# Layer 1's value projection for four head pairs in one 512-column pass at the layer junction, the keys' copied half on VectorE, and background sums held one step

## The chip, the cores and the metric

The kernel runs on one core of a Trainium2 chip. The metric is the device time of one execution in microseconds (us); lower is better. Engines are named as the profile names them: PE is TensorE (matmuls; PEld is its weight load), DVE is VectorE, ACT is ScalarE, POOL is GpSimd, and SP is SyncE, which here only issues the DMA transfers. Each engine works through its own instructions strictly in their order; between engines there are only semaphores.

## The reference

Two decoder layers on a residual stream of 512 tokens by 1024, float32, 16 heads of 64. Layer 0 has stick-breaking attention, layer 1 forgetting attention. Cut to what matters here:

```python
h = modulate(rmsnorm(x, g_mix_pre[i]), sh_a, sc_a)
q, k, v = (split_heads(t) for t in split(h @ w_qkv[i], 3))     # w_qkv: 1024 x 3072
if i == 0:
    o = stick_breaking_attention(q, k, v)
else:
    log_f = log_sigmoid(h @ w_fg + b_fg)                       # 16 columns
    o = softmax(q.k * scale + cum[t] - cum[s], causal) @ v     # cum = cumsum(log_f)
x = x + gt_a * rmsnorm(o @ w_o[i], g_mix_post[i])
h = modulate(rmsnorm(x, g_ffn_pre[i]), sh_f, sc_f)
x = x + gt_f * rmsnorm((silu(conv3(h @ w_gate)) * (h @ w_up)) @ w_down, g_ffn_post[i])
```

The six vectors `sh_a ... gt_f` of a layer are `silu(c) @ w_mod[i] + b_mod[i]`, each a 1024 x 1024 product with one vector.

## The kernel before

**Arithmetic.** To keep float32 accuracy every operand is split into a rounded high part and a low part (`split`, L245: ACT copies, then DVE or POOL subtracts), and a product is three matmuls into one PSUM bank (`mm3`, L318): high by high (L320), high by low (L321), low by high (L322). All are 128 x 128 weights against at most 512 moving columns.

**Weights.** One list (`ws`, L289) has every weight tile of the program in the order in which it is needed. A tile is 512 KB: a load into `wf` (three buffers) from SP, then its split into `wh` and `wl` (three buffers each, `w_tile`), or into four 128 x 512 pieces of the pool `slot` (`w_slots`; 44 slots, shared with attention's tiles and the feed-forward's results `ys`). Asking for a tile (`ws.need`) also issues the next ones, two ahead where nothing else is said. Of the qkv and output weights the low parts are made by POOL, of the feed-forward weights by DVE.

**Order.** PE and SP run in the order of the Python code. DVE, ACT and POOL are put in order by a scheduler when the program is built; only layer 0's start is in code order there too.

**The junction.** Layer 0 ends with the down projection. Its last four weight tiles are kept in slots and run token block by token block (four blocks of 128), so that a block's norms (`postnorm`, then `scaled`, each with a power of -0.5 on POOL, L333) run while the next block is multiplied. `finish_next` turns a finished block into layer 1's input `ht` (8 transposes on PE into `pt`, L373, then ACT and DVE). Layer 1 then begins with the values of head pairs 0 and 1 (`values`, group 0: 256 columns, for each block 8 x 3 matmuls of 256 moving columns), mixed with the last two blocks' transposes (`ready(2)`, `ready(3)`), the first half of q of pair 0, the forget gates (`forget`, 16 matmuls into `pf`, then a chain over ACT, DVE, a DRAM buffer `cumd` and the tiles `cum`), the rest of q (L835) and k (L836) of pair 0. The values of group 1 (pairs 2 and 3) come later, among the fillers.

**Attention.** `attention` (L574) works head by head; `UNITS` (L32) says for each head how many filler units (three matmuls of 512 columns, or six of 256) PE runs between its scores, transposes and sums. The fillers are the projections of the next pairs, values of later groups, and parts of the output projection. `keys` (L426) makes k of a pair: ACT rounds each head's half into `kh` (L431), POOL copies that half to the other 64 partitions (L433), DVE makes the low half `kl` (L434).

**Background sums.** During the feed-forward of layer 0 six modulation vectors are computed as background (`mod_part`, L133): eight loads `wm` from the pool `t4` (three buffers), each followed by a DVE multiply-add into `acc` (L144, L146); then `acc` is split into `ah` (ACT, L149) and `al` (DVE, L151), both in `t4` as well, and four matmuls `pm` (L163, L164) sum over partitions. `bg.step(4)` after each of the 22 feed-forward blocks (L928) runs four yields of this.

## Time and profile before

| what | value |
|---|---|
| time, median of 3 runs (lowest to highest) | 1272.24 us (1270.95 to 1272.52) |
| the profiled execution's own time | 1271.76 us |
| its span, first to last instruction | 1270.0 us |
| granted TensorE clock, mean | 0.999 |
| PE busy | 1246.4 us, 98% of the span |
| PEld, DVE, ACT, POOL busy | 81%, 54%, 47%, 21% |

The profiled execution is 0.48 us below the median; 1.8 us of its time lie outside the span. Matmuls overlap in the profile: a matmul of 512 columns is shown as some 0.39 us long while the next one starts 0.23 us after it. So what a matmul costs is the distance between starts, and an idle time shown in brackets hides a further 0.16 us (0.39 - 0.23) of lost spacing. The kernel is computed by PE almost without a pause, so its time is PE's spacing plus the few places where PE waits.

### The profile page before, as it was taken

The numbers are of one execution on the slowest core, as the hardware profiler recorded it, in microseconds if no ns is written. First come the engines' busy times: TensorE is split into PE (matmuls) and PEld (weight loads), VectorE is DVE, ScalarE is ACT, GpSimd is POOL, SyncE is SP. The second block draws the span as 40 slices with busy tenths as digits, with TensorE's granted clock in tenths as the row PEclk, the third lists the DMA queues.
The fourth block names the chain that finished last, engine by engine and source line by source line (L and its number), as shares of the span: only waits on it lengthen the run. The fifth ranks groups of instructions, "written<-read, shape, count | busy, mean of one in ns | idle before, by whom it ended". The sixth has DMA issues, their size and how long they took to land.

```text
span 1270.0 us, 17006 instructions
## 1 busy us (share of the span) xinstructions
PE 1246.4 (98%) x6380; PEld 1026.5 (81%) x6380; DVE 681.3 (54%) x1157; ACT 601.6 (47%) x1149; POOL 267.5 (21%) x302
## 2 busy tenths in 40 slices
PE   6999999999999999999999999999999999999997
PEld 5877878789887888888887888877988888888886
DVE  6655444377688887422263654554685444442233
ACT  7577667565333334311375655565743333332121
POOL 5764444610000000000215554352000000000000
PEclk9999999999999999999999999999999999999999
DMA  9746334324587875333504443233073333332331
GB/s 298 216 145 218 124 93 157 100 67 167 166 249 225 267 217 170 91 95 98 151 1 130 122 133 115 90 128 101 22 244 102 98 100 100 100 96 89 97 100 67
DMA packets 178357, 169.71 MB, mean 134 GB/s; under 512 B 6983, under 2 KB 151775, under 8 KB 178274
## 3 DMA queue, kind: packets, MB, share of 16 engines
q1 hardware_dynamic: 178098, 168.56, 43.5%
q8 instruction: 50, 0.82, 0.3%
q14 instruction: 33, 0.27, 0.1%
q10 hardware_dynamic: 176, 0.07, 0.0%
HBM read 166.44 MB, written 2.16 MB: 133 GB/s over the span
## 4 chain that ended last, share of the span: by engine, by line
PE 83%; DVE 6%; DMA 4%; ACT 4%; issue 1%; POOL 1%; SPq 0%; DVEq 0%; ACTq 0%; POOLq 0%
PE pgu L321 11%; PE pgu L322 11%; PE pgu L320 11%; PE pd L322 6%; PE pd L321 6%; PE pd L320 6%; PE pqk L320 4%; PE pqk L322 4%; PE pqk L321 4%; PE ps L442 3%; PE po L493 3%; PE pv L320 3%; PE pa L478 3%; PE pv L321 3%; PE pv L322 3%; DMA wf<-in_w_ffn_up_dram 2%
## 5 line engine op out<-in xcount | busy, mean ns | idle before, releaser
L246 ACT CAST wh<-wf 128x1024 fp32r<-128x1024 f32 (+2 forms) x178 | 185.3, 1041 | 307.6 <-PE pd L322 134.4
L321 PE MATMUL pgu<-htl,wh 128*128 128x512 f32 (+1 forms) x736 | 276.4, 376 | 0.6 <-DVE htl L382 0.6
L320 PE MATMUL pgu<-hth,wh 128*128 128x512 f32 (+1 forms) x736 | 276.3, 375 | 0.0
L322 PE MATMUL pgu<-hth,wl 128*128 128x512 f32 (+1 forms) x736 | 276.1, 375 | 0.0
L247 DVE TENSOR_TENSOR wl<-wf,wh 128x1024 fp32r<-128x1024 f32 x122 | 149.2, 1223 | 214.5 <-ACT wh L246 212.2
L321 PEld LDWEIGHTS pgu<-htl,wh 128*128 128x128 f32 x736 | 138.5, 188 | 26.2 <-DVE htl L382 1.0
L322 PEld LDWEIGHTS pgu<-hth,wl 128*128 128x128 f32 x736 | 138.5, 188 | 24.9
L320 PEld LDWEIGHTS pgu<-hth,wh 128*128 128x128 f32 x736 | 138.5, 188 | 24.9
L247 POOL TENSOR_TENSOR wl<-wf,wh 128x1024 fp32r<-128x1024 f32 (+3 forms) x56 | 129.7, 2320 | 122.4 <-ACT wh L246 101.6
L333 POOL TENSOR_TENSOR r<-v,mhalf 128x1 f32<-128x1 f32 x32 | 17.6, 551 | 450.5 <-DVE v L329 450.5
L320 PE MATMUL pd<-wh,yh 128*128 128x512 f32 x288 | 112.0, 389 | 0.0
L321 PE MATMUL pd<-wl,yh 128*128 128x512 f32 x288 | 112.0, 389 | 0.0
L322 PE MATMUL pd<-wh,yl 128*128 128x512 f32 x288 | 112.0, 389 | 0.0
L320 PE MATMUL pqk<-hth,wh 128*128 128x512 f32 (+1 forms) x240 | 99.6, 415 | 0.0
L322 PE MATMUL pqk<-hth,wl 128*128 128x512 f32 (+1 forms) x240 | 92.6, 386 | 0.9 <-POOL wl L247 0.9
L321 PE MATMUL pqk<-htl,wh 128*128 128x512 f32 (+1 forms) x240 | 92.5, 385 | 0.0
L904 ACT ACTIVATE cv<-cv 128x512 f32<-128x512 f32 x44 | 27.8, 632 | 111.1 <-DVE cv L903 103.8
L146 DVE SCALAR_TENSOR_TENSOR acc<-wm,csil,acc 128x1024 f32<-128x1024 f32 x52 | 66.6, 1281 | 16.5 <-DMA wm<-in_w_mod_dram 16.0
L320 PE MATMUL pv<-wh,hth 128*128 128x256 f32 (+1 forms) x224 | 70.8, 316 | 1.2 <-ACT hth L690 1.2
L322 PE MATMUL pv<-wh,htl 128*128 128x256 f32 (+1 forms) x224 | 66.9, 299 | 0.0
L321 PE MATMUL pv<-wl,hth 128*128 128x256 f32 (+1 forms) x224 | 66.7, 298 | 0.0
L321 PEld LDWEIGHTS pd<-wl,yh 128*128 128x128 f32 x288 | 54.1, 188 | 11.3
(208 smaller groups left out, 2241.0 us busy)
## 6 DMA issues: line engine op xcount, KB each, us to landing
wm<-in_w_mod_dram SPq DMA_DIRECT2D x80, 512.0 KB, 6.1
wf<-in_w_ffn_gate_dram SPq DMA_DIRECT2D x44, 512.0 KB, 4.9
wf<-in_w_ffn_up_dram SPq DMA_DIRECT2D x44, 512.0 KB, 4.7
wf<-in_w_ffn_down_dram SPq DMA_DIRECT2D x44, 512.0 KB, 3.5
wf<-in_w_qkv_dram SPq DMA_DIRECT2D x41, 512.0 KB, 5.8
wm<-in_w_mod_dram SPq DMA_DIRECT2D x32, 256.0 KB, 5.7
wf<-in_w_o_dram SPq DMA_DIRECT2D x16, 512.0 KB, 3.6
cum<-cumd SPq DMA_DIRECT2D x16, 512.0 KB, 5.4
```

Source lines behind the costliest of these rows:

```text
L146: nc.vector.scalar_tensor_tensor(acc, w, csil[:, d : d + 1], acc, op0=ALU.mult, op1=ALU.add)
L246: nc.scalar.copy(hi, src)
L247: (engine or nc.vector).tensor_tensor(lo, src, hi.bitcast(F32), op=ALU.subtract)
L320: nc.tensor.matmul(ps, ah, bh, start=first, stop=False)
L321: nc.tensor.matmul(ps, ah, bl, start=False, stop=False)
L322: nc.tensor.matmul(ps, al, bh, start=False, stop=last)
L333: nc.gpsimd.tensor_tensor(r, v, mhalf, op=ALU.pow)
L442: nc.tensor.matmul(ps[:, :n], q[hd][:, qs], k[hd][i][:, :n], start=i == 0, stop=i == 1)
L478: nc.tensor.transpose(ps[:, (qb - kb) * P : (qb - kb + 1) * P], probs[qb][:, kb * P : (kb + 1) * P], idn)
L493: nc.tensor.matmul(po[HD * hd : HD * hd + HD, kb * P :], vt[p // 4, kb][:, e : e + HD], at[hd][kb], start=kb == 0, stop=kb == NT - 1, tile ...
L904: nc.scalar.activation(a, a, AF.Silu)
```

## The change

Four parts.

1. **Values of four pairs.** In layer 1, groups 0 and 1 become one projection of 512 columns (`values4`): for each block 8 x 3 matmuls of 512 moving columns, its weights loaded as four tiles into 16 slots with the low parts on POOL. The order at the junction becomes values of block 0, transposes of block 2, values of block 1, transposes of block 3, values of block 2, forget gates, all of q and k of pair 0 (no longer in two halves), values of block 3. The four loads are asked for earlier (at block 1 of the down projection's end), and the two `ws.need` calls with 0 ahead limit how far the list runs on.
2. **Fillers.** Without group 1 there are 16 filler units fewer, and layer 1's `UNITS` go from 185 to 169 in sum, 18 to 14 for head 0, 12 to 10 or 11 for heads 1 to 8.
3. **Keys.** In both layers DVE fills the other 64 partitions of `kh` straight from PSUM; POOL's copy is gone.
4. **Background sums.** After `ah` and `al` the part yields `True`, which ends the step. So `pm` stands behind the next feed-forward block on PE. A part takes three steps where it took 2.75.

```diff
-         [18, 12, 12, 12, 12, 12, 13, 12, 12, 12, 11, 9, 10, 10, 4, 9, 5]]
+         [14, 10, 10, 10, 10, 11, 11, 11, 12, 12, 11, 9, 10, 10, 4, 9, 5]]
...
             res = cst.tile([P, ND], F32, name=nm("mc"))
-        yield
+        yield True
         for h in range(2):
...
         def step(self, n=1):
+
             while n and self.gens:
                 try:
-                    next(self.gens[0])
-                    n -= 1
+                    n = 0 if next(self.gens[0]) else n - 1
                 except StopIteration:
                     self.gens.pop(0)
...
-            vs = [((l, "v", p // 2, i), wq[:, 4 * i : 4 * i + 4, 2 * D + p * P : 2 * D + p * P + 256], 256) for i in range(2) if p % 2 == 0]
+            vs = [((l, "v", p // 2, i), wq[:, 4 * i : 4 * i + 4, 2 * D + p * P : 2 * D + p * P + 256], 256) for i in range(2) if p in (4, 6)]
+            if (l, p) == (1, 0):
+                for i in range(4):
+                    src = wq[:, 2 * i : 2 * i + 2, 2 * D : 2 * D + 512]
+                    ws.add((l, "v4", i), lambda src=src: w_slots(src, 512, nc.gpsimd))
...
         for (hi, lo), own, other in zip(res, (A, B), (B, A)):
-            nc.gpsimd.tensor_scalar(hi[other], hi[own].bitcast(F32), 1.0, 1.0, op0=ALU.mult, op1=ALU.mult)
+            nc.vector.tensor_copy(hi[other], ps[own])
             nc.vector.tensor_tensor(lo[own], ps[own], hi[own].bitcast(F32), op=ALU.subtract)
...
+    def values4(l, t, ht, vt):
+
+        ps = bank("pv")
+        for d in range(ND):
+            w = ws.need((l, "v4", d // 2), 4 - d // 2)
+            mm3(ps, block(ht, d, t * P, (t + 1) * P), w[d % 2], d == 0, d == ND - 1)
+        vt[0, t] = slot("v", F32)
+        nc.scalar.copy(vt[0, t], ps)
...
         else:
-            drain(values(l, 0, 0, ht, vt))
+            values4(l, 0, ht, vt)
             ready(2)
-            drain(values(l, 0, 1, ht, vt))
-            first = proj(l, 0, 0, ht, scale, qk, ((0, 256), (256, 512)))
-            for _ in range(4):
-                next(first)
+            ws.need((l, "qk", 0, 1), 0)
+            values4(l, 1, ht, vt)
             ready(3)
-            drain(values(l, 0, 2, ht, vt))
-            if l % 2:
-                cums_of[l] = forget(ht)
-            drain(values(l, 0, 3, ht, vt))
-            drain(first)
-            drain(proj(l, 0, 1, ht, None, qk))
+            ws.need((l, "qk", 1, 0), 0)
+            values4(l, 2, ht, vt)
+            cums_of[l] = forget(ht)
+            for j, s in ((0, scale), (1, None)):
+                drain(proj(l, 0, j, ht, s, qk))
+            values4(l, 3, ht, vt)
...
-            if p % 2 == 0 and p >= (4 if l == 0 else 2):
+            if p in (4, 6):
                 gens += [values(l, p // 2, t, ht, vt) for t in range(NT)]
...
                 xn[t] = scaled(t)
+                if t == 1:
+                    ws.need((l + 1, "v4", 3), 0)
```

What the built program's order shows at three places (names are the program's with their numbers; line numbers of the changed kernel are 4 to 13 higher).

POOL at the end of layer 0's down projection, before: `wl` are the low parts of the first three qkv tiles, `kl` the cleared key tiles, `r_1169` and `r_1175` the first two powers of -0.5, for block 0's norms.

```order
L423 MEMSET kl_1230_6011 64x512
L423 MEMSET kl_1231_6012 64x512
L423 MEMSET kl_1232_6013 64x512
L423 MEMSET kl_1233_6014 64x512
L247 TENSOR_TENSOR wl_1158_5754<-wf_1156_5751,wh_1157_5753 128x1024
L247 TENSOR_TENSOR wl_1161_5766<-wf_1159_5763,wh_1160_5765 128x1024
L247 TENSOR_TENSOR wl_1236_6022<-wf_1234_6019,wh_1235_6021 128x1024
L333 TENSOR_TENSOR r_1169_5787<-v_1168_5785,mhalf_78 128x1
L333 TENSOR_TENSOR r_1175_5799<-v_1174_5797,mhalf_78 128x1
```

The same place now; six more `sl` (low parts of the four value tiles) stand ahead of the first row.

```order
L247 TENSOR_TENSOR sl_1203_5878<-wf_1201_5875,sh_1202_5877 128x512
L247 TENSOR_TENSOR sl_1205_5882<-wf_1201_5875,sh_1204_5881 128x512
L427 MEMSET kl_1244_6039 64x512
L427 MEMSET kl_1245_6040 64x512
L247 TENSOR_TENSOR wl_1251_6051<-wf_1249_6048,wh_1250_6050 128x1024
L427 MEMSET kl_1246_6041 64x512
L427 MEMSET kl_1247_6042 64x512
L247 TENSOR_TENSOR wl_1259_6107<-wf_1257_6104,wh_1258_6106 128x1024
L247 TENSOR_TENSOR wl_1268_6164<-wf_1266_6161,wh_1267_6163 128x1024
L337 TENSOR_TENSOR r_1173_5795<-v_1172_5793,mhalf_78 128x1
```

Block 0's first power stands behind eight half tiles, three whole ones and four clears, where it stood behind three whole tiles.

POOL at k of pair 7 in layer 0, before, with what each instruction waits for:

```order
L247 TENSOR_TENSOR wl_554_2532<-wf_552_2529,wh_553_2531 128x1024 [waits PE_49,DMAHW3_49,Activation_49,Pool_49]
L433 TENSOR_SCALAR kh_548_2519<-kh_548_2519 64x512 [waits Activation_49,Pool_49]
L433 TENSOR_SCALAR kh_549_2520<-kh_549_2520 64x512 [waits Activation_49]
L247 TENSOR_TENSOR sl_558_2551<-wf_556_2548,sh_557_2550 128x512 [waits DMAHW4_49,Activation_49,Pool_49]
L247 TENSOR_TENSOR sl_560_2555<-wf_556_2548,sh_559_2554 128x512 [waits Activation_49]
```

DVE at the same k now:

```order
L437 CAST kh_548_2519<-pqk_528_2424 64x512 [waits PE_49,Activation_49]
L438 TENSOR_TENSOR kl_6_101<-pqk_528_2424,kh_548_2519 64x512
L437 CAST kh_549_2520<-pqk_528_2424 64x512
L438 TENSOR_TENSOR kl_7_102<-pqk_528_2424,kh_549_2520 64x512
L221 TENSOR_REDUCE mc_438_2002<-pm_555_2541 128x4 [waits PE_49]
```

The copy has moved from behind a weight's low part on POOL to DVE, where the two low halves stood alone, and it waits for ACT.

SP in layer 0's feed-forward around the first background sum, before (`gp` is loaded at the yield behind `ah` and `al`, `wm` is the next part's):

```order
L156 DMA gp_785_3671<-in_g_ffn_post_dram 128x1024
L142 DMA wm_789_3682<-in_w_mod_dram 128x1024
L252 DMA wf_792_3687<-in_w_ffn_gate_dram 128x8x128
L252 DMA wf_795_3717<-in_w_ffn_up_dram 128x8x128
L142 DMA wm_801_3757<-in_w_mod_dram 128x1024
L142 DMA wm_802_3760<-in_w_mod_dram 128x1024
L142 DMA wm_803_3763<-in_w_mod_dram 128x1024
L142 DMA wm_804_3766<-in_w_mod_dram 128x1024
```

The same place now:

```order
L156 DMA gp_785_3671<-in_g_ffn_post_dram 128x1024
L252 DMA wf_788_3675<-in_w_ffn_gate_dram 128x8x128
L252 DMA wf_791_3705<-in_w_ffn_up_dram 128x8x128
L142 DMA wm_800_3754<-in_w_mod_dram 128x1024
L142 DMA wm_801_3757<-in_w_mod_dram 128x1024
L252 DMA wf_804_3762<-in_w_ffn_gate_dram 128x8x128
L252 DMA wf_807_3792<-in_w_ffn_up_dram 128x8x128
L142 DMA wm_813_3832<-in_w_mod_dram 128x1024
```

One feed-forward block's two weight loads now come ahead of the next part's first `wm`, which came ahead of them.

## Rows read from the trace of the kernel before

**Rows 1.** The page, part 1: busy time of each engine.
```profile
PE 1246.4 (98%) x6380; PEld 1026.5 (81%) x6380; DVE 681.3 (54%) x1157; ACT 601.6 (47%) x1149; POOL 267.5 (21%) x302
```

**Rows 2.** PE's timeline: start, us, operation, [idle before <- what ended it].
```profile
224.18 0.50 PE L442 MATMUL ps<-kh,qa 128*128 128x512 f32 x1 [1.58 <-POOL kh L433]
...
393.55 0.50 PE L163 MATMUL pm<-ah,ones 128*128 128x512 f32 x1 [0.40 <-ACT ah L149]
395.39 0.50 PE L164 MATMUL pm<-al,ones 128*128 128x512 f32 x1 [1.34 <-DVE al L151]
...
661.62 1.09 PE L373 MATMUL pt<-zid,xn 128*128 128x128 f32 x8 [0.76 <-DVE xn L363]
...
681.94 0.50 PE L442 MATMUL ps<-kh,qa 128*128 128x512 f32 x1 [1.45 <-POOL kh L433]
682.49 0.50 PE L442 MATMUL ps<-kl,qa 128*128 128x512 f32 x1
...
696.04 0.50 PE L322 MATMUL pqk<-hth,wl 128*128 128x512 f32 x1 [0.86 <-POOL wl L247]
```

**Rows 3.** PE's timeline: 512-column matmuls, then 256-column ones, without waits.
```profile
642.69 0.39 PE L320 MATMUL pd<-sh,yh 128*128 128x512 f32 x1
...
647.00 0.39 PE L321 MATMUL pd<-sl,yh 128*128 128x512 f32 x1
...
651.06 0.28 PE L320 MATMUL pv<-wh,hth 128*128 128x256 f32 x1
...
653.82 0.28 PE L322 MATMUL pv<-wh,htl 128*128 128x256 f32 x1
```

**Rows 4.** POOL's and DVE's timelines at pair 7's keys, layer 0.
```profile
221.06 2.37 POOL L247 TENSOR_TENSOR wl<-wf,wh 128x1024 fp32r<-128x1024 f32 x1 [2.52 <-ACT wh L246]
223.51 1.31 POOL L433 TENSOR_SCALAR kh<-kh 64x512 fp32r<-64x512 f32 x2
...
222.05 1.41 DVE L434 TENSOR_TENSOR kl<-pqk,kh 64x512 fp32r<-64x512 f32 x2 [1.95 <-ACT kh L431]
```

**Rows 5.** DVE's groups by form, from PSUM and from SBUF.
```profile
L434 DVE TENSOR_TENSOR kl<-pqk,kh 64x512 fp32r<-64x512 f32 x30 | 20.6, 687 | 10.1 <-ACT kh L431 9.7
L381 DVE CAST hth<-hf 128x512 fp32r<-128x512 f32 x12 | 5.1, 422 | 4.5 <-ACT hf L378 4.5
```

**Rows 6.** The waits: engine, operation <- waited for: us in total, times, longest.
```profile
DVE u L388 <- ACT junk L341: 34.6, 8, 14.0
```

**Rows 7.** POOL's groups by form.
```profile
L247 POOL TENSOR_TENSOR wl<-wf,wh 128x1024 fp32r<-128x1024 f32 x47 | 112.6, 2402 | 116.8 <-ACT wh L246 96.6 <-PE pa L478 8.8 <-PE pv L321 5.6
L247 POOL TENSOR_TENSOR sl<-wf,sh 128x512 fp32r<-128x512 f32 x20 | 25.4, 1297 | 19.3 <-ACT sh L246 17.2 <-issue 1.9
...
L423 POOL MEMSET kl<- 64x512 f32 x8 | 4.2, 524 | 95.2 <-PE pd L321 94.9
```

**Rows 8.** ACT's timeline: the first qkv tile of layer 1 has landed.
```profile
619.94 1.05 ACT L246 CAST wh<-wf 128x1024 fp32r<-128x1024 f32 x1 [1.50 <-DMA wf<-in_w_qkv_dram]
```

**Rows 9.** POOL's, DVE's and PE's timelines: block 0 at the junction.
```profile
634.77 0.55 POOL L333 TENSOR_TENSOR r<-v,mhalf 128x1 f32<-128x1 f32 x1 [3.53 <-DVE v L329]
...
638.54 0.88 DVE L363 TENSOR_SCALAR xn<-xs,r 128x512 f32<-128x512 f32 x2 [0.67 <-POOL r L333]
...
641.12 1.03 PE L373 MATMUL pt<-zid,xn 128*128 128x128 f32 x8
```

**Rows 10.** DVE's timeline: layer 1's first softmax row block.
```profile
689.63 0.69 DVE L463 CUSTOM_DVE_ANT_0 fx<-ps,cum 128x512 f32<-128x512 f32 x1 [6.47 <-POOL cum L549]
```

**Rows 11.** Layer 0's feed-forward: a stretch (us, busy of PE, PEld, DVE, ACT, POOL, clock, DMA).
```profile
380.00:400.00 20.00, 18.26 (x80) 14.57 (x79) 18.08 (x26) 7.07 (x9) 0.00 (x0) 1.00 0.75 222
```

**Rows 12.** DVE's timeline and the DMA issues (count, KB each, median us to landing).
```profile
399.04 1.22 DVE L247 TENSOR_TENSOR wl<-wf,wh 128x1024 fp32r<-128x1024 f32 x1
...
wm<-in_w_mod_dram SPq DMA_DIRECT2D x80, 512.0 KB, 6.1
wf<-in_w_ffn_gate_dram SPq DMA_DIRECT2D x44, 512.0 KB, 4.9
```

## The prediction

> **What bounds the kernel now.** I read the page first: PE is busy 1246.4 us of a span of 1270.0, and no other engine over 54% [rows 1]. So a change gains only by shortening what PE has to do or by removing one of its pauses. The 23.6 us of pause are few and large; I looked for them in PE's timeline. About 9 us lie in layer 0's start and 7 at the very end, which this change does not touch. The rest, but for three of about 0.3 us, is in [rows 2]: a wait for POOL's copied half of k at pair 7 of layer 0 and again at pair 0 of layer 1, a wait for a background sum's `ah` and `al`, one for block 3's `xn` at the junction, one for a weight's low part early in layer 1's attention. As the section on the profile says, each costs its bracket and 0.16 of hidden spacing.
>
> **1. Width.** In [rows 3] the two 512-column matmuls are 19 starts apart, 4.31/19 = 0.227 us each; the two 256-column ones 23 starts apart, 2.76/23 = 0.120. Groups 0 and 1 of the values were 2 x 96 = 192 matmuls of 256 and become 96 of 512: 192 x 0.120 - 96 x 0.227 = 23.04 - 21.79 = **1.25**. The first q loses its halves: 48 x 0.120 - 24 x 0.227 = **0.31**. Nothing hides these, PE is the bound: 1.56 gained. By the Trainium skill (TensorE: Matmul & The Clock Gate, Back-to-back issue gap) a warm matmul's spacing is its columns at 2.4 GHz and about 2.5 ns, which is 109 and 216 ns. By that rule both terms would be 0.3 together; this trace has 120 and 227, and the measured spacing decides.
>
> **2. The junction's order.** Between block 2's and block 3's transposes stand 5.45 us of values now (24 x 0.227), where 24 + 24 matmuls of 256 stood (5.76), but block 2's come 2.57 later than before behind block 0's values, and block 3's chain no longer has block 2's subtraction of 1.1 us ahead of it on DVE. The wait for `xn`, 0.76 + 0.16 = **0.92** [rows 2], should go; behind it nothing is late. If block 3 is late by all that block 2's new place gives, up to 0.9 comes back.
>
> **3. Keys.** At pair 0 of layer 1 the scores waited 1.45 + 0.16, and 682.49 - 681.94 - 0.227 = 0.32 for `kl` [rows 2]. Now 5.45 us of block 3's values stand between k's projection and the scores. DVE needs four operations, at most 4 x 0.69 = 2.8, behind ACT's two copies: hidden, **1.93** gained.
> At pair 7 of layer 0 nothing new stands between. POOL's copies began at 223.51, behind a weight's low part that ran from 221.06 [rows 4]; DVE was free for `kl` at 222.05. The new copy isn't in the trace. Its bounds are DVE's 0.69 from PSUM and 0.42 for a cast from SBUF [rows 5]; I take 0.69, since it reads the same bank in the same shape. `kh` is ready at 222.74 and `kl` at 223.44, so the second score matmul starts there and not at 224.18 + 0.34: **1.07** gained; with 0.42 it is 1.34. The copy waits for ACT's two copies of the same bank, as DVE's product waits for ACT's square of the same bank elsewhere [rows 6]. The Trainium skill (PSUM — Partial Sum Buffer, PSUM bank collisions raise a hardware error) says why: two engines must not touch one bank in the same 32 partitions at once, two reads included. By that rule the gain is the 1.07; if the two could read together the whole wait of 1.74 would go. The row bears the rule out.
> In all other pairs PE did not wait for k, and DVE's 2 x 0.69 a pair lie beside fillers; an uncovered one would cost at most 0.7.
>
> **4. Background sums.** `pm` waited 0.40 + 0.16 and then 395.39 - 393.55 - 0.227 = 1.61: **2.17** [rows 2]. A feed-forward block is 48 x 0.227 = 10.9 us of PE, so a sum that is asked for one block later is there. What would be late next: the weights. DVE is busy 18 of 20 us there [rows 11], and the next block's second tile gets its low part at 399.04 + 1.22 = 400.26 [rows 12]; PE asked for it one tile of 24 matmuls and the brackets after `pm`, 395.39 + 0.34 + 24 x 0.227 + 0.45 = 401.6, and would 2.17 earlier, at 399.4. So between 0 and 2.17 stays. A part now takes three steps and not 2.75, so DVE and the DMA have 8% less background work in a block; I take the whole, 2.17.
>
> **5. Fillers.** The 16 units of group 1 move from attention to the junction; their cost is in part 1. Heads get some 1.4 us shorter. The heads behind the eighth had 9 to 11 units before and no pause over 0.35, so nothing for that. The wait of 0.86 + 0.16 = **1.02** for a low part [rows 2] came because head 0 ran 18 units, two of them with pair 2's q; now it runs 14, of pair 1 alone, and that tile has a head more. Against it, `forget` comes later: three times 5.45 - 2.88, less 2.88 of q and the 0.92, is 3.9, and 3.3 from part 6. The first softmax then starts not at 689.63 [rows 10] but near 696.8. PE starts head 0 some 10.7 later too, and its transposes need the rows a head later. I cost this at 0, up to 1 if the chain is slower.
>
> **6. What it costs: POOL at the junction.** The order shows that POOL does all low parts of four value tiles and three q and k tiles, and four clears, before block 0's first power: 8 x 1.297 + 3 x 2.402 + 4 x 0.524 = 19.7 us [rows 7]. It can't start sooner than the first tile lands, 619.94 [rows 8], and ACT's half copy is done, about 620.5: SP's first three loads wait for buffers of the down projection as before. So the power comes at 640.2 and not at 634.77 [rows 9], 5.4 later. From the power to the first half of `xn` the chain took 638.54 + 0.44 - 634.77 = 4.2, so PE can transpose block 0 at 644.4, where it did at 641.12. PE loses **3.3**. The later blocks' chains follow at the distances they had and just fit. The ends: 2.9 if POOL is a little quicker, 5 if it also waits for tiles.
>
> **Sum.** 1.56 + 0.92 + 1.93 + 1.07 + 2.17 + 1.02 = 8.67 gained, 3.3 lost, 5.4 net. Against the profiled execution's 1271.76 that is 1266.4; against the median, 0.48 above it, **1266.8 us**.
>
> **The rivals.**
> *POOL's queue is hidden after all.* If the tiles are split earlier than the rows allow, or block 0 has more room, the 3.3 do not come: 1272.24 - 8.7 = 1263.5. For it: `xn` of block 0 was ready 2.1 us ahead of PE [rows 9] (638.98 against 641.12), so a delay up to that costs nothing. Against it: POOL's work alone is 19.7 us behind a landing that the trace gives.
> *The pause only moves.* The sum's wait becomes a wait for weights (400.26 against 399.4, part 4), or the chains behind POOL miss by another one or two microseconds: 2 to 4 of the gain go, 1269 to 1271.
> *Slower.* SP is one queue. While `ah` and `al` are held for a block more, two of the three `t4` buffers are taken, and the next part's second `wm` must wait for the first to land and be added, 6.1 + 1.3 = 7.4 us [rows 12], with the feed-forward's `wf` behind it. A weight tile that is asked for one block ahead has 10.9, less 4.9 to land [rows 12] and 2.3 to split: 3.7 of room. So a part could cost 7.4 - 3.7 = 3.7. It decides from the second such part on; three of the five would give 1266.8 + 11.1 = 1278. Against it: in this stretch `wf` was loaded more than a block ahead, and `wm` waited for buffers before, too.
>
> **How the numbers follow.** 0.2% of 1272 is 2.5 us, about what a measurement of this kernel can tell from no change, so faster means below 1269.7. The forecast gets 0.52 (1265.5 to 1268), the hidden queue 0.13, the moving pause 0.27, of which a little under half is below 1269.7, slower 0.08. That gives faster 0.77, same 0.15, slower 0.08. The range 1263.0 to 1271.0 leaves out the slower case, the edge of the moving pause and half of the hidden queue.
>
> **What would show it.** Of the new profile: PE without waits at k in layer 1 and at `pm`; a wait of about half a microsecond at pair 7; block 0's transposes with a wait of 3 us for `xn`, itself behind POOL's power near 640; 512-column `pv` matmuls 0.227 apart. The prediction is wrong if POOL's power comes before 637, if PE waits for `wh` or `wl` between 340 and 500, or if the transposes of head 0's rows wait.

## The result, and the profile after

The changed kernel takes **1274.78 us** (median of 10 runs, 1274.21 to 1277.61) where the kernel before, on the same chip, takes 1271.66 (10 runs, 1270.95 to 1273.72). The ratio is 1.0028 with a 95% interval of 1.0020 to 1.0036: slower by about 3 us, or 0.3%. The forecast was 1266.8 and faster. The profiled execution of the changed kernel took 1276.54 us, 1.8 above its median; its span is 1274.8. Of the ten runs, the six from 1274.21 to 1274.84 list a mean granted clock of 0.998 (one of them 0.996), and the four from 1276.01 up, the profiled one among them, 0.993 to 0.996.

The page's part 1 of the changed kernel, answering to [rows 1]:

```profile
PE 1249.6 (98%) x6260; PEld 1023.1 (80%) x6260; DVE 704.7 (55%) x1189; ACT 601.8 (47%) x1149; POOL 248.4 (19%) x274
```

PE has 120 instructions fewer and is still busy 3.2 us longer. The pauses of [rows 2] are all shorter or gone: pair 7 of layer 0 has two small ones, and at `pm`, at the first `xn` of block 3, at pair 0 and at 696 nothing is left. In their place PE's timeline of the changed kernel has these (columns as in [rows 2]; first pair 7, then the junction, then layer 1's third head, then its last heads):

```profile
223.12 0.49 PE L446 MATMUL ps<-kh,qa 128*128 128x512 f32 x1 [0.17 <-DVE kh L437]
223.83 0.50 PE L446 MATMUL ps<-kl,qa 128*128 128x512 f32 x1 [0.22 <-DVE kl L438]
...
642.72 1.77 PE L377 MATMUL pt<-zid,xn 128*128 128x128 f32 x8 [4.36 <-DVE xn L367]
644.14 0.77 PE L324 MATMUL pd<-sh,yh 128*128 128x512 f32 x1
644.72 0.63 PE L325 MATMUL pd<-sl,yh 128*128 128x512 f32 x1
645.14 0.63 PE L326 MATMUL pd<-sh,yl 128*128 128x512 f32 x1
...
714.16 0.47 PE L446 MATMUL ps<-kh,qa 128*128 128x512 f32 x1 [1.38 <-DVE kh L437]
714.79 0.50 PE L446 MATMUL ps<-kl,qa 128*128 128x512 f32 x1 [0.15 <-DVE kl L438]
...
717.14 0.33 PE L482 MATMUL pa<-zid,fx 128*128 128x128 f32 x1 [0.94 <-DVE fx L472]
717.88 0.33 PE L482 MATMUL pa<-zid,fx 128*128 128x128 f32 x1 [0.41 <-DVE fx L472]
...
852.63 0.33 PE L482 MATMUL pa<-zid,fx 128*128 128x128 f32 x1 [0.42 <-DVE fx L472]
854.59 0.38 PE L446 MATMUL ps<-kh,qa 128*128 128x256 f32 x1 [0.26 <-ACT at L488]
855.67 0.33 PE L446 MATMUL ps<-kh,qa 128*128 128x128 f32 x1 [0.36 <-ACT at L488]
```

With 0.16 added for each bracket, as the section on the profile says, the junction costs 4.52 us (4.36 + 0.16), the third head 3.61 (1.54 + 0.40 + 1.10 + 0.57, where the second term is the 0.63 between the starts at 714.16 and 714.79 less a normal 0.227) and the last heads 1.52 where one wait of 0.51 stood before.

The rows behind the junction's pause show a second cost: the 512-column matmuls at 644.72 and 645.14 are 0.42 us apart instead of 0.227. Windows of the same trace give the granted clock (columns as in [rows 11]; the clock is the number behind POOL's entry, 0.66 and 0.79 here; 1.00 is 2.4 GHz, 0.50 is 1.2 GHz):

```profile
642.00:647.00 5.00, 4.28 (x16) 3.71 (x17) 3.56 (x7) 1.87 (x6) 0.69 (x2) 0.66 0.00 0
714.00:722.00 8.00, 6.34 (x22) 4.70 (x23) 6.58 (x18) 4.34 (x11) 3.55 (x3) 0.79 0.40 133
```

After the 4.36 us of idling PE ran at the lower level for the eight transposes and five matmuls: about 1.7 us lost (0.63 on the transposes, 1.05 on the matmuls, against the same forms at full clock). At the third head it fell again behind the last of the four waits, from 717.96 to 721.6 by the spacing of the matmuls. I estimate that loss at 1.5, from the same forms at full clock.

Who made the junction late is read from ACT, POOL and DVE in front of 642.72:

```profile
616.77 1.14 ACT L246 CAST sh<-wf 128x512 fp32r<-128x512 f32 x2 [1.17 <-DMA wf<-in_w_qkv_dram]
...
632.56 1.06 ACT L246 CAST wh<-wf 128x1024 fp32r<-128x1024 f32 x1 [2.01 <-DMA wf<-in_w_qkv_dram]
633.52 0.29 ACT L246 CAST fgp<-fgw 128x128 fp32r<-128x128 f32 x1
633.71 0.59 ACT L345 ACTIVATE junk<-pd 128x512 bf16<-128x512 f32 x1
```

```profile
617.47 10.05 POOL L247 TENSOR_TENSOR sl<-wf,sh 128x512 fp32r<-128x512 f32 x8 [110.22 <-ACT sh L246]
...
632.17 4.74 POOL L247 TENSOR_TENSOR wl<-wf,wh 128x1024 fp32r<-128x1024 f32 x2
638.42 0.55 POOL L337 TENSOR_TENSOR r<-v,mhalf 128x1 f32<-128x1 f32 x1 [1.50 <-DVE v L333]
```

```profile
633.84 3.23 DVE L247 TENSOR_TENSOR fgp<-fgw,fgp 128x128 fp32r<-128x128 f32 x1 [17.43 <-ACT fgp L246]
636.99 1.28 DVE L392 TENSOR_TENSOR u<-pd,gt 128x512 f32<-128x512 f32 x2
```

Three things stand in block 0's way. ACT's square of block 0 (`junk`, 633.71) is in its queue behind the rounding of the third qkv tile, which waited for its load; in the kernel before, the square waited for PE. POOL's subtractions and clears run to 636.91 with hardly a gap. And DVE's `fgp` (the low part of the forget gates' weights), 0.29 us long in the kernel before, took 3.23 and ended 0.16 after POOL's second `wl`; block 0's product `u` stands behind it. The power of -0.5 came 1.5 us after POOL was free, because of `fgp`.

### The profile page after: what moved, and what is told of

Its sections match the earlier page's. It is cut to its first block, busy times and chain, and to the rows that moved or that the text cites. A ratio compares the mean times of both kernels' runs of the same rounds, so it can differ in the third digit from the quotient of the medians.

```text
span 1274.8 us, 16733 instructions
## 1 busy us (share of the span) xinstructions
PE 1249.6 (98%) x6260; PEld 1023.1 (80%) x6260; DVE 704.7 (55%) x1189; ACT 601.8 (47%) x1149; POOL 248.4 (19%) x274
## 4 chain that ended last, share of the span: by engine, by line
PE 90%; DVE 4%; ACT 2%; DMA 2%; POOL 1%; issue 1%; ACTq 0%; DVEq 0%; POOLq 0%
PE pgu L325 13%; PE pgu L326 13%; PE pgu L324 12%; PE pd L324 6%; PE pd L325 5%; PE pd L326 5%; PE pqk L324 4%; PE pqk L325 4%; PE pqk L326 4%; PE ps L446 3%; PE po L497 3%; PE pv L324 3%; PE pv L325 3%; PE pv L326 3%; PE pa L482 3%; PE po L324 1%
## 5 line engine op out<-in xcount | busy, mean ns | idle before, releaser
L246 ACT CAST wh<-wf 128x1024 fp32r<-128x1024 f32 (+2 forms) x174 | 181.1, 1041 | 277.7 <-PE pd L326 128.8
L247 POOL TENSOR_TENSOR wl<-wf,wh 128x1024 fp32r<-128x1024 f32 (+3 forms) x52 | 119.9, 2310 | 108.6 <-ACT wh L246 106.0
L324 PE MATMUL pqk<-hth,wh 128*128 128x512 f32 x232 | 99.0, 427 | 0.0
L326 PE MATMUL pqk<-hth,wl 128*128 128x512 f32 x232 | 91.6, 395 | 0.0
L325 PE MATMUL pqk<-htl,wh 128*128 128x512 f32 x232 | 91.6, 395 | 0.0
L326 PEld LDWEIGHTS pd<-wh,yl 128*128 128x128 f32 x288 | 54.1, 188 | 11.3
L324 PEld LDWEIGHTS pd<-wh,yh 128*128 128x128 f32 x288 | 54.1, 188 | 11.2
L247 POOL TENSOR_TENSOR sl<-wf,sh 128x512 fp32r<-128x512 f32 x28 | 35.5, 1297 | 132.4 <-ACT sh L246 132.3
```

The lines of the kernel that those rows point to most:

```text
L246: nc.scalar.copy(hi, src)
L247: (engine or nc.vector).tensor_tensor(lo, src, hi.bitcast(F32), op=ALU.subtract)
L324: nc.tensor.matmul(ps, ah, bh, start=first, stop=False)
L325: nc.tensor.matmul(ps, ah, bl, start=False, stop=False)
L326: nc.tensor.matmul(ps, al, bh, start=False, stop=last)
```

## The experiments

Differences in us are medians against the kernel before, timed together with it; by that measure the changed kernel is at +3.1. "Less than the changed kernel" is the distance between two such differences.

**The sums alone.** The kernel before with part 4 only:

```diff
-        yield
+        yield True
...
-                    next(self.gens[0])
-                    n -= 1
+                    n = 0 if next(self.gens[0]) else n - 1
```

> The kernel before, with the background sums held a step and nothing else changed. Theory (the waits for ah and al are the whole of it, and no weight comes late in their place): PE's 0.56 and 1.61 us at the first sum go, 2.2 us less than before, 1269.5 us where before has 1271.7. Rival (the next weight's low part takes the place of the sum, as layer 0's feed-forward is short of room): a wait for wl of 1 to 2 us appears after the sum, and the time is 1270.5 to 1272.

1270.26 against 1272.31, ratio 0.9983 (0.9974 to 0.9991): **-2.05**. PE has no wait at `pm` and none for weights between 340 and 500, neither here nor in the changed kernel. The theory held; this part did what it was costed at.

**The keys alone.** The kernel before with DVE's copies only (`nc.vector.tensor_copy(hi[other], ps[own])` for POOL's).

> The kernel before, with k's copied half by VectorE in both layers and nothing else changed. Theory (VectorE's copies are harmless while layer 1's first softmax has the room that the kernel before gives it): pair 7 of layer 0 loses 0.5 us instead of 1.75, pair 0 of layer 1 about 0.7 less than its 1.93, no wait of over 0.5 at pair 1: 1.5 to 2.5 us less than before, 1269.2 to 1270.2. Rival (the copies stand in VectorE's queue behind the softmax and hold the next head's scores whatever the start): a wait of over 1 us for kh or kl at pair 1 or a later pair of layer 1 and waits for fx behind it, and no gain: 1271 to 1273.

1273.04 against 1272.31, ratio 1.0005 (0.9996 to 1.0014): **no difference** that can be measured, so the gain that the theory had is not there; nor is the rival's wait at pair 1. Its PE rows at layer 1's pair 0 and last heads:

```profile
682.14 0.49 PE L442 MATMUL ps<-kh,qa 128*128 128x512 f32 x1 [1.98 <-DVE kh L433]
682.85 0.50 PE L442 MATMUL ps<-kl,qa 128*128 128x512 f32 x1 [0.22 <-DVE kl L434]
...
848.73 0.33 PE L478 MATMUL pa<-zid,fx 128*128 128x128 f32 x1 [0.42 <-DVE fx L468]
850.69 0.39 PE L442 MATMUL ps<-kh,qa 128*128 128x256 f32 x1 [0.26 <-ACT at L484]
851.77 0.33 PE L442 MATMUL ps<-kh,qa 128*128 128x128 f32 x1 [0.36 <-ACT at L484]
```

At pair 0 the wait grew from 1.45 to 1.98 [rows 2]: DVE's copies and products come one after the other, while POOL copied beside DVE's product. In layer 1's last heads, where few fillers are left, the additional DVE work put 1.0 us on the path. Against these losses of some 1.7 stand the gain at pair 7 (0.92) and the wait at 696 (1.02), which went. Why it went is open: POOL's low part there began 0.75 sooner, but in the kernel before POOL was idle for 3.4 us between its copies and its next subtraction, so the copies weren't what held it.

**v4's low parts on DVE** (v4 is the four 512-column value tiles of `values4`). The changed kernel with

```diff
-                    ws.add((l, "v4", i), lambda src=src: w_slots(src, 512, nc.gpsimd))
+                    ws.add((l, "v4", i), lambda src=src: w_slots(src, 512))
```

> The changed kernel, with the low parts of the four 512-column value tiles made by VectorE, which is idle there from 616 to 634 us, instead of POOL. Theory (POOL holds the three load buffers: its eight subtractions and four clears set when the last qkv tile lands, ScalarE has that tile's rounding ahead of block 0's squares, and VectorE's fgp is stretched to 3.2 us beside POOL's subtraction): ScalarE's last wh lands 3 or more us sooner, PE's wait of 4.36 for xn falls under 1.0 and with it the stretch of clock 0.83, 5 to 6 us less than the changed kernel. Rival (the loads themselves are late, whoever makes the low parts): wh lands within 1 us of 632.6, the wait stays above 3 us, and the time is within 1.5 us of the changed kernel's.

1272.29 against 1272.31: **3.1 less** than the changed kernel, ratio to before 1.0000 (0.9991 to 1.0009). Between theory and rival. Its PE, ACT and DVE:

```profile
641.07 0.66 PE L377 MATMUL pt<-zid,xn 128*128 128x128 f32 x4 [2.32 <-DVE xn L367]
...
631.18 1.05 ACT L246 CAST wh<-wf 128x1024 fp32r<-128x1024 f32 x1 [1.45 <-DMA wf<-in_w_qkv_dram]
632.33 0.59 ACT L345 ACTIVATE junk<-pd 128x512 bf16<-128x512 f32 x1
...
632.46 2.96 DVE L247 TENSOR_TENSOR fgp<-fgw,fgp 128x128 fp32r<-128x128 f32 x1 [6.93 <-ACT fgp L246]
```

Half of the pause is gone, not all: seven loads in a row still bring the last tile at 631.2, only 1.4 sooner, ACT's square still stands behind it, and `fgp` still takes 2.96 beside POOL's last two subtractions. POOL's queue was a part of the cause. Not all of the 3.1 lies at the junction: the wait of 1.38 for `kh` at the third head is gone in this run too (0.15 for `kl` is left), while both waits for `fx` stay.

**fgp early.** The changed kernel with the forget gates' weights loaded and split ahead of the down projection:

```diff
+        if l == 0:
+            fg = gates()
         banks = [[bank("pd"), bank("pd")] for _ in range(NT)]
...
-            cums_of[l] = forget(ht)
+            cums_of[l] = forget(ht, *fg)
```

> The changed kernel, with the forget gates' weights loaded and split ahead of layer 0's down projection instead of at the junction (fgp leaves ScalarE's and VectorE's queues there). Theory (VectorE's fgp, stretched from 0.29 to 3.2 us beside POOL's subtraction, stands ahead of block 0's u): the first power on POOL comes when its queue is empty, near 636.9 instead of 638.4, PE's wait for xn falls from 4.4 to about 3, 1 to 2 us less than the changed kernel. Rival (POOL's queue or ScalarE's casts alone set the pause, fgp is covered): the wait stays above 4.0.

1273.79 against 1272.13: **1.5 less** than the changed kernel. POOL, DVE and PE:

```profile
632.68 4.75 POOL L247 TENSOR_TENSOR wl<-wf,wh 128x1024 fp32r<-128x1024 f32 x2
637.53 0.55 POOL L337 TENSOR_TENSOR r<-v,mhalf 128x1 f32<-128x1 f32 x1
...
635.16 2.29 DVE L333 SCALAR_TENSOR_TENSOR v<-m,m 128x1 f32<-128x1 f32 x1
...
641.83 0.44 PE L377 MATMUL pt<-zid,xn 128*128 128x128 f32 x2 [3.10 <-DVE xn L367]
```

The theory held: the pause is 3.10 + 0.16, and the power now comes 0.1 us after POOL's last subtraction, so POOL's queue sets it. (The wait for `kh` at the third head also fell, from 1.38 to 1.02.) The DVE row is a surprise: `v`, an operation on 128 numbers that takes 0.15 us elsewhere, took 2.29 and ended 0.02 after POOL.

**v4 early.** The changed kernel with the four tiles in the list between the down projection's tiles 11 to 14 instead of ahead of pair 0's, low parts on DVE:

```diff
+            if l == 0 and 11 <= f < 15:
+                src = w_qkv[1].rearrange("(d p) e -> p d e", p=P)[:, 2 * (f - 11) : 2 * (f - 11) + 2, 2 * D : 2 * D + 512]
+                ws.add((1, "v4", f - 11), lambda src=src: w_slots(src, 512))
...
-            w = halves(ws.need((l, "dn", f)))
+            w = halves(ws.need((l, "dn", f), 4 if l == 0 and 9 <= f < 16 else 2))
...
-            w = ws.need((l, "v4", d // 2), 4 - d // 2)
+            w = ws.need((l, "v4", d // 2), 0)
...
-                    ws.need((l + 1, "v4", 3), 0)
+                    ws.need((l + 1, "qk", 0, 0), 0)
```

> The changed kernel, with the four 512-column value tiles moved in the list of weights between the down projection's tiles 11 to 14 (some 35 us sooner, where the DMA engines are a third busy), their low parts by VectorE. Only three qkv tiles are left at the junction, as before. Theory (the seven loads and their subtractions in one row behind the down projection made the pause): ScalarE's square of block 0 no longer stands behind a cast, PE's wait for xn falls under 0.5 and the slow clock behind it is gone: 5 to 7 us less than the changed kernel, 2 to 4 less than with the low parts alone moved to VectorE. Rival (block 0 comes 3 us sooner and the chain of norms itself is too long for the next block's 5.4 us): a wait of 2 us or more for xn stays.

1268.76 against 1272.13, ratio 0.9973 (0.9962 to 0.9983): **6.5 less** than the changed kernel. PE, ACT, DVE and POOL at block 0:

```profile
639.24 1.03 PE L376 MATMUL pt<-zid,xn 128*128 128x128 f32 x8
...
630.59 0.60 ACT L344 ACTIVATE junk<-pd 128x512 bf16<-128x512 f32 x1 [3.70 <-PE pd L325]
...
622.25 0.29 DVE L247 TENSOR_TENSOR fgp<-fgw,fgp 128x128 fp32r<-128x128 f32 x1 [4.94 <-ACT fgp L246]
...
632.89 0.55 POOL L336 TENSOR_TENSOR r<-v,mhalf 128x1 f32<-128x1 f32 x1 [3.48 <-DVE v L332]
```

The square waits for PE again, `fgp` is 0.29 long, POOL is idle ahead of the power, PE's transposes wait for nothing, and the clock is 1.00 from 640 to 650. The theory held in full: the pause and the clock behind it were the seven loads with their low parts in one row. About 0.5 of the 6.5 lies elsewhere: the wait for `kh` at the third head fell from 1.38 to 0.83.

**The sums undone.** The changed kernel with `yield` for `yield True`.

> The changed kernel with the background sums as before, and nothing else changed: PE comes to the junction some 2.2 us later. Theory (the loads there start when the down projection's tiles free their buffers, so they move with PE, and what is gained ahead of the junction is kept): the wait for xn stays at 4 us or more, and the time is 2 us above the changed kernel's, near 1276.8. Rival (the chain of loads and low parts ends at its own time, and the pause swallows what PE gained ahead of it): the wait shrinks by about 2 us and the time stays within 0.7 us of the changed kernel's.

1277.06 against 1272.21, 1.7 more than the changed kernel, ratio to before 1.0037 (1.0024 to 1.0050). PE:

```profile
644.40 0.63 PE L377 MATMUL pt<-zid,xn 128*128 128x128 f32 x3 [4.38 <-DVE xn L367]
```

The pause stays at 4.38 though PE comes 1.7 later, and POOL's first low part of v4 came 1.7 later with it (619.19 instead of 617.47): the work at the junction moves with PE. That the down projection's buffers tie the two together is read from the order of the loads and not tested by itself. What is gained ahead of the junction is kept.

**Keys of layer 1 on POOL.** The changed kernel with POOL's copy in layer 1, DVE's in layer 0:

```diff
-            nc.vector.tensor_copy(hi[other], ps[own])
+            if l:
+                nc.gpsimd.tensor_scalar(hi[other], hi[own].bitcast(F32), 1.0, 1.0, op0=ALU.mult, op1=ALU.mult)
+            else:
+                nc.vector.tensor_copy(hi[other], ps[own])
```

> The changed kernel, with the keys' copied half by POOL again in layer 1 (VectorE keeps it in layer 0). The junction's pause of 4.5 us stays. Theory (layer 1's first heads are short because the softmax starts 4 to 10 us later against the fillers; POOL's copy too stands behind a low part of 2.4 us that ends at 712.7): the wait at pair 1's first scores stays at 1.2 to 2 us, only the waits for fx at 717 fall, by up to 1.4: 1 to 2 us less than the changed kernel. Rival (VectorE's copies in the softmax's queue are the whole cost): the wait at pair 1 falls under 0.5 and none for fx is left: 3 to 4 us less than the changed kernel.

1271.99 against 1272.31: **3.4 less** than the changed kernel, with the junction's pause at 4.78. The rival is nearly right: the wait for `kh` is 0.30, though two small ones for `fx` are left:

```profile
714.45 0.50 PE L449 MATMUL ps<-kh,qa 128*128 128x512 f32 x1 [0.30 <-POOL kh L438]
716.56 0.33 PE L485 MATMUL pa<-zid,fx 128*128 128x128 f32 x1 [0.22 <-DVE fx L475]
717.30 0.33 PE L485 MATMUL pa<-zid,fx 128*128 128x128 f32 x1 [0.41 <-DVE fx L475]
```

**Units.** The changed kernel with 18 and 12 units for layer 1's first two heads (9 for head 2, 10 for heads 3 to 7, 11 for heads 8 and 9, which the change had left at 12; the sum stays 169).

> The changed kernel with layer 1's filler units given back to the first two heads (18 and 12 instead of 14 and 10, heads 2 to 9 one or two fewer; the sum is the same 169). Theory (the softmax of layer 1's first heads, which starts late behind forget, stands ahead of pair 1's keys on VectorE, and the heads are too short to hide it): the waits at pair 1 (1.5 and 0.4) and for fx (1.1 and 0.6) go, with them the second stretch of slow clock: 3 to 5 us less than the changed kernel. Rival (VectorE's two more operations for each pair are the cost, whatever the heads' length): the waits move to another head and less than 1.5 us is gained.

1271.66 against 1272.13: **3.6 less** than the changed kernel; no wait at the third head and full clock there, while the junction has its 4.46. So two different mends remove most of the same waits. How the 14 units make them is seen in ACT, DVE and POOL. In the changed kernel PE ended pair 1's k at 705.4 (the 48th `pqk` matmul behind the first scores), two units into head 1; ACT has it behind head 1's softmax (`fx`), and DVE behind more of it:

```profile
707.83 0.72 ACT L470 ACTIVATE fx<-fx,mx 128x512 f32<-128x512 f32 x1 [2.19 <-DVE mx L467]
...
710.72 1.17 ACT L435 CAST kh<-pqk 64x512 fp32r<-64x512 f32 x2
...
711.05 1.86 DVE L472 TENSOR_SCALAR fx<-fx,rc 128x384 f32<-128x384 f32 x1
...
713.34 0.68 DVE L437 CAST kh<-pqk 64x512 fp32r<-64x512 f32 x1
...
710.29 2.40 POOL L247 TENSOR_TENSOR wl<-wf,wh 128x1024 fp32r<-128x1024 f32 x1 [1.45 <-ACT wh L246]
```

With 18 units k is done within head 0, and its copies come first: ACT's at 707.25 and DVE's

```profile
708.46 0.68 DVE L437 CAST kh<-pqk 64x512 fp32r<-64x512 f32 x1 [0.88 <-ACT kh L435]
...
710.55 0.69 DVE L438 TENSOR_TENSOR kl<-pqk,kh 64x512 fp32r<-64x512 f32 x1
...
714.74 0.42 DVE L472 TENSOR_SCALAR fx<-fx,rc 128x384 f32<-128x384 f32 x1
```

7 us before PE needs them at 718.10. My theory for this run (the softmax starts late behind `forget`) is not what happened: the first row block's maximum came at 694.04, 1.5 us behind PE's first scores, where 7.7 us lay between before (689.63 [rows 10] and 681.94 [rows 2]). It is the 14 units that cut pair 1's k in two.

A third thing stands in these rows. DVE's `fx` of 384 columns of head 1, which stands ahead of k's copy here, is 1.86 us long beside POOL's `wl`; in the run with 18 units it is 0.42. In all eight profiles with 14 units it is 1.85 to 1.87 long, in all three with 18 units 0.41 or 0.42. So up to 1.4 of the wait for `kh` is this stretch, which the 14 units make together with POOL's subtraction; no run takes it away by itself.

**v4 and units alone.** The kernel before with parts 1 and 2, sums and keys as they were.

> The kernel before with the value tiles, the order at the junction and the filler units changed, and nothing else (sums and keys as before). Theory (each part keeps its own price: the sums alone gave 2.0, the keys lose 2 to 3 in layer 1 and gain 1.3 at pair 7): 1 to 2.5 us slower than before, 1273 to 1274.5, a wait for xn of 4 us or more. Rival (the pause at the junction is made by PE's coming 3.2 us sooner, not by the loads): the wait is under 2 us and the kernel is 1 to 3 us faster than before.

1276.57 against 1272.21, ratio 1.0035 (1.0022 to 1.0048): **+4.4**, more than expected. The pause at the junction is there with PE at its old pace, and a little larger. At the third head PE waits for POOL's `kh` here, and 0.22 and 0.41 for `fx`:

```profile
647.30 0.69 PE L377 MATMUL pt<-zid,xn 128*128 128x128 f32 x2 [5.01 <-DVE xn L367]
...
719.83 0.50 PE L446 MATMUL ps<-kh,qa 128*128 128x512 f32 x1 [1.02 <-POOL kh L437]
```

So parts 1 and 2 alone lose more than the whole change. The single prices add up (+4.4, -2.05 for the sums, +0.7 for the keys is +3.0, where the changed kernel is at +3.1), but the +0.7 is within the noise and the parts aren't independent: in the changed kernel DVE's copies in layer 1 cost 3.4.

**Mends together.** v4 early, and layer 1's keys on POOL:

> Both mends together: the value tiles early as above, and the keys' copied half on POOL in layer 1, VectorE in layer 0. If the junction and layer 1's keys were the two places where the change lost, it is now faster than before by the gains of the prediction: sums 2.0, pair 7 1.3, width 1.6, xn 0.9, the wait at pair 0 about 1.9, the wait at 696 about 0.8, together 8.5 and less about 1 for what is left in layer 1's first heads: 1264 to 1266 us where before has 1272.3. Rival (the loads among the down projection make PE wait there, or layer 1's first softmax is short again because block 0 comes sooner): 1267 to 1271.

1265.22 against 1272.13, ratio 0.9943 (0.9929 to 0.9957). Waits of 0.57, 0.22 and 0.41 were left at the third head. With the units of heads 0 and 1 as well:

> The value tiles early, the keys' copied half on POOL in layer 1, and the filler units of heads 0 and 1 at 18 and 12 (the sum stays 169). Theory (the waits of 0.7, 0.4 and 0.6 us that were left in layer 1's third head are all the short first heads'): they go, 1.3 to 2 us less than without the units, 1263 to 1264 us. Rival (the fillers taken from heads 2 to 9 are missed there): the waits move and the time stays at 1265.

**1263.43 us** against 1272.21, ratio **0.9933** (0.9919 to 0.9947), 8.8 us faster than before and 11.9 than the changed kernel: the best kernel of this study. The page's part 1:

```profile
PE 1243.9 (99%) x6260; PEld 1020.0 (81%) x6260; DVE 698.7 (55%) x1181; ACT 601.4 (48%) x1149; POOL 247.8 (20%) x282
```

And the same with DVE's copies in layer 1 as well, to price the keys alone where the heads have room:

> The same with the keys' copied half on VectorE in layer 1 as well, so that only the keys differ from the run beside it. Theory (once the first heads are long enough, VectorE's copies cost only at layer 1's last heads, near 850 us, where PE waited 0.59, 0.43 and 0.52 with them and 0.50 without, and 0.7 at pair 0 if that is uncovered): 1.0 to 1.8 us slower than with POOL, 1264.5 to 1265.5. Rival (with room the two are the same): within 0.5 us of each other.

1265.32, **1.9 more** than with POOL, timed together with it. The last heads have 0.43, 0.25 and 0.36 where POOL's version has one wait of 0.33: 1.0 of the 1.9. The rest is not in any wait of over 0.25 us and stays open.

With the value tiles early, all four pairings of units and keys were timed (us against the kernel before):

| layer 1's units of heads 0 and 1 | DVE's copies in layer 1 | POOL's copies in layer 1 |
|---|---|---|
| 14 and 10 | -3.4 | -6.9 |
| 18 and 12 | -6.9 | -8.8 |

Either mend is worth 3.5 where the other is missing and 1.9 where it is there. So the loss at the third head belongs to the short heads and DVE's copies together, and neither can be charged with it alone.

## Why the prediction was wrong

Against the forecast for the profiled execution, 1266.4, the measured 1276.54 is 10.1 too long. The gains came as forecast. What failed are the costs: the fillers of part 5, put at 0, the keys of layer 1 in part 3, put at nothing past pair 0, and the junction of part 6, where the mechanism was right and the size half of what it measured. By the steps of the prediction:

- **Width, the waits at xn, pair 0 and 696, the sums (parts 1 to 5).** Right. None of these waits is left in the changed kernel, the sums alone gave 2.05 where 2.17 stood, and pair 7 lost 0.83 instead of 1.75, a gain of 0.92 where 1.07 stood. The 512-column `pv` matmuls are 0.227 apart as forecast (654.83 to 656.87, nine starts), though the width was not timed alone. The sum of the gains was 8.67; the kernel in which all three losses are mended is 8.78 faster than before. That is near the rival of the hidden queue, 1263.5, only that the changed kernel didn't hide it. So close an agreement is in part luck: that kernel has POOL's copies in layer 1 and other units, and of the terms only the sums were timed by themselves.
- **POOL at the junction (part 6).** Its queue was sized well: 19.44 us from 617.47 to 636.91, where 19.7 stood. Both ends of the comparison came 3 us sooner than written (ACT's first rounding began at 616.77, PE was ready at 638.20 = 642.72 - 4.52). The prediction had left its own gains ahead of the junction out of both; that they cancel, since both ends move with PE (the run with the sums undone), was luck and not foresight. With `fgp` out of the way the pause is 3.26, the forecast's 3.3. What the step missed is what else stands in the queues beside POOL. DVE's `fgp` was held until POOL's subtraction ended: 4.52, 1.2 more. And PE's clock fell behind the pause: 1.7. So the term was 6.2, not 3.3; v4 early gave back 6.5, of which 0.5 is at the third head.
- **Fillers (part 5).** The step that failed most. "It runs 14, of pair 1 alone" was written as a gain; that pair 1 has sixteen units, so that two of them fall into head 1 and k ends behind head 1's softmax in ACT's and DVE's order, was not followed. I costed it at 0, up to 1. It was 3.6 of waits and, in the profiled execution, some 1.5 of slow clock; the units given back return 3.6. What the step weighed instead, a late `forget`, did not make PE wait: head 0's transposes waited for nothing. The loss at the third head is shared with the next step.
- **Keys (part 3).** "In all other pairs PE did not wait for k, and DVE's 2 x 0.69 a pair lie beside fillers" fails twice (an uncovered operation was priced at 0.7 at most). At the third head DVE's copies and the short heads make the waits together: POOL's copies alone return 3.4, as the units alone do 3.6. And at the end of layer 1, where fillers run out, they cost 1.0 in waits, 1.9 in the timed pair of runs. It was priced for the scores that wait for k and not for the softmax that stands behind the copies on DVE.
- **The slower rival.** It did not happen: no weight was waited for in the feed-forward. The prediction gave a slower kernel 0.08, and for this reason alone; the loss came from three other places that it had at 3.3 together.

Added up: 1.2 at the wait, 1.7 and 1.5 of clock, 3.6 at the third head, 1.0 at the last heads, 0.15 at pair 7 is some 9.2 of the 10.1. Matched matmul by matmul, the two traces confirm where it lies: the changed kernel is 2.9 us ahead at 515.79, 3.3 behind at 646.41 after the slow stretch, 3.2 behind at 850.91 ahead of the last heads and 4.8 behind at 906.46, as at the end. The other 0.9 is some 0.2 in the first 15 us and small differences elsewhere. The median run is 1.8 shorter than the profiled one and lists the higher clock, so it has less of the slow stretches; which of the two can't be told. The runs with fgp early and v4 early, with waits of 1.0 and 0.8 us for `kh` at the third head, don't have the second.

The sign that I named for the junction ("POOL's power near 640, a wait of 3 us") came almost true: 638.42 and 4.36. The price behind it was short. The sign "PE without waits at k in layer 1" failed at the third head. None of the three signs of being wrong came: the power was after 637, PE waited for no weight between 340 and 500, and head 0's transposes didn't wait (those that did are head 1's). They watched the places that the prediction had in mind, and the loss lay beside them.

## What to carry to other kernels

When a burst of weight loads moves to a point where a serial chain on small engines begins, list everything that the burst puts ahead of that chain on each in-order engine, the rounding that waits for the last load too, and look for idle DMA time before it: four tiles loaded 33 to 44 us sooner, their low parts on another engine, gave back 6.5 us. When filler counts change, find in which head each projection now ends and what stands ahead of its evacuation; here two units that fell into the next head cost 3.6 us, together with two more operations on DVE. Price an operation that goes to another engine also by what stands behind it there, in the stretch with the fewest fillers.

## What the runs showed of the hardware

**DVE waits for POOL.** Some DVE operations end just when a POOL subtraction ends, whatever their size: `fgp` 633.84 + 3.23 = 637.07 where POOL ended at 636.91; `v` 635.16 + 2.29 = 637.45 where POOL ended at 637.43; `fx` 711.05 + 1.86 = 712.91 where POOL's `wl`, 710.29 to 712.69, ran. Others did not: DVE's products from PSUM ran beside POOL at their usual 0.69. It could be read in the trace before, from DVE and POOL of layer 1's second head:

```profile
702.96 2.08 DVE L468 TENSOR_SCALAR fx<-fx,rc 128x512 f32<-128x512 f32 x1
...
702.34 2.42 POOL L247 TENSOR_TENSOR wl<-wf,wh 128x1024 fp32r<-128x1024 f32 x1
```

The Trainium skill (SBUF — State Buffer, Summary: rules for kernel authors) has the rule: a DVE operation in a two-port mode (both of DVE's SBUF port pairs) and a POOL operation exclude each other, and so do a DVE operation with two SBUF inputs and a POOL operation that reads SBUF; the second to start waits until the first ends. The rows agree, though the profile doesn't show in which mode `fx` ran. They add that `fgp` (two SBUF inputs) did not get in between two POOL operations in a row: it came during the first `wl` of a pair and ended only behind the second, in the changed kernel (3.23), in the run with v4's low parts on DVE (2.96) and with the sums undone (4.10, from 634.65 to 638.75 beside POOL's 633.86 to 638.60). An `fx` (one SBUF input, 128x384) did get in between: in the changed kernel it ran from 778.35 to 780.21, POOL's first `wl` from 777.59 to 780.00, and the second took 2.53 instead of 2.39. What decides between the two was not tested.

**The clock after a pause.** Idling for 4.36 us took PE from 2.4 to 1.2 GHz for 3.7 us after it, 1.7 lost; 2.32 us did so too, in the run with v4's low parts on DVE (matmuls 0.43 apart from 642.7 to 644.9). With 18 units a pause of 4.46 was followed by 5.6 us at the lower level (642.70 to 648.30), so the price of one pause varies. The pauses of [rows 2], up to 1.58, left the clock at 1.00. A forecast of a pause of 3 us has to carry this price.
